# First mixer of a two-layer encoder: queries and keys of the next head traced ahead of the value products and the closing of a head, its values and scores behind them

## The chip, the cores and the metric

The kernel runs on one core of a Trainium2 chip. The metric is the device time of one execution in microseconds (us). The engines are TensorE (PE; its weight loads PEld), VectorE (DVE), ScalarE (ACT), GpSimd (POOL) and SyncE (SP), which here issues the transfers.

## The reference

An encoder of two layers, width 1024, runs on two sequences, a sample of 512 tokens and a prompt of 256, 768 tokens together. Each layer is a mixer and a convolutional feed-forward block, both with a conditioning (`adaln`) that scales, shifts and gates. The mixer of the first layer is a two-way mLSTM with 4 heads of 256 channels; the change is in it. Cut to what matters:

```python
proj = h @ w_in                       # q, k, v, o: 1024 channels each; 16 gate channels
s   = einsum('td,sd->ts', qc, kc) * exp(log_d - m_t)
num = einsum('ts,se->te', s, vc) + (state of earlier chunks)
den = sum(s) + (state of earlier chunks)
h   = num / maximum(abs(den), exp(-m_t))
hs  = h_fwd + h_bwd
hs  = hs * rsqrt(mean(hs * hs) + EPS) * head_g
return (hs * sigmoid(o)) @ w_out
```

All is computed in float32. The second layer has windowed attention as its mixer.

## The kernel before

**Precision.** Each float32 operand is split into a high and a low part (`fp_copy_split`, L232 to L240: ScalarE casts the high part, VectorE subtracts for the low one), and each product is three matmuls: high by high, high by low, low by high. Activations lie in `hh` and `hl` (tiles `zh`, `zl`), weights come as units of 256 output channels. `halves` (L257) loads a unit in two half-units of 128x1024 into the tag `raw` (5 buffers, L244) and splits them into `whi` and `wlo` (3 buffers each).

**Products.** `gemmT` (L265) makes 128 output channels of one half-unit for one sequence, channels on partitions: 24 matmuls of 512 columns for the sample, 24 of 256 for the prompt. `gemmN` (L308) makes values, tokens on partitions: 6 tiles of 24 matmuls. Both write PSUM banks of the tag `ps` (4 banks); scores, value products and transposes use the tag `pa` (4 banks).

**The mixer** (`mlstm`, L737). After the opening norm, the gates and the queries of head 0, a loop runs over the heads h (L795). For each it traces, in this order:

1. the masks `mb` (L797): two loads of gate rows on SP (L800) and two additions on POOL (L802);
2. the queries and keys (L808 to L822): two units, four half-units, eight calls of `gemmT`, evacuated by a split with or without a scale (`keep`, L753; ScalarE L236 or L239, VectorE L237 or L240);
3. the scores (L845 to L880): for each of 4 + 2 key blocks the products `S`, the weights `E` by ScalarE's exponentials (L864 to L868), VectorE's multiplications (L869, L870) and the split into `PT` (sample) or `nt` (prompt);
4. the values (`values`, L824): ahead of the scores in head 0, behind them in the others;
5. the closing (L887 to L932): the value products of scores and `v`; denominators (ACT L908, DVE L911 and L912); scaling and sum of the two directions (ACT L913, DVE L914); squares with a sum (ACT L916); the root by a power (DVE L918, POOL L919); the scaling by it (ACT L922); transposes (PE L926) and the evacuation into `hsT` (DVE L930).

Behind the loop four units of `o` are made by `gemmT`, put through a sigmoid (ACT L942), multiplied by `hsT` (POOL L943) and split into `ho` (L934 to L944). The output projection reads `ho`.

**Side work.** Two generators are advanced at fixed points: `fill` (L818, L832, L940), the conditioning of layer 1, whose step is two multiply-adds of 128x1024 on VectorE (L470, L472); and `fillp` (L820, L834, L890), that of layer 0, whose step is four matmuls of 256 columns with 32 weight columns. Both load rows of 512 KB into `raw`, and both take a `ps` bank for a group of eight rows.

**Memory.** `slab` (L220) is a tag of 6 buffers for the large tiles. While a head's scores run, its masks, queries, keys and values and one or two `hsT` tiles hold slabs.

**What sets the order.** A scheduler at build time (L1716, `schedule_with_timeline_sim=True`) puts the instructions of each engine into a fixed order, along a timeline that it simulates: of two instructions that are ready, the one that was traced first goes first. Where the code traces a step is thus its priority, and an instruction traced later can be put ahead of one that is not ready in the simulated timeline. `issue_after` (L842, L852) keeps head 0's scores behind its values. On the chip each engine works through its fixed order.

Of the kernel before, what the change touches and what calls it, by code (L numbers as in the profile page):

```python
# [10 lines left out]
F32 = mybir.dt.float32  # L11
R = mybir.dt.float32r
AF = mybir.ActivationFunctionType
ALU = mybir.AluOpType

P = 128
D = 1024
KC = D // P
T = 768
# [46 lines left out]
U_MIN = 0  # L66
# [79 lines left out]
class Net:  # L146
# [590 lines left out]
    def mlstm(self, pool, xt, rows, raws):  # L737
        nc, io = self.nc, self.io
        T6 = T // P
# [5 lines left out]
        F, a, M, z = (B[0:G, j] for j in range(4))  # L745
# [39 lines left out]
        aT = pool.tile([P, T6, G], F32, name="aT")  # L785
        eT = pool.tile([P, T6, G], F32, name="eT")

        def columns(src, dst):
            pt = self.pa()[:, : T6 * G]
            for t in range(T6):  # L790
                nc.tensor.transpose(pt[:, t * G : (t + 1) * G], src[:, t * P : (t + 1) * P], self.ident[0:G, 0:G])
            nc.vector.tensor_copy(dst, pt.rearrange("p (t g) -> p t g", g=G))

        hsT = [self.slab([P, 4, T]) for _ in range(2)]
        for h in range(4):  # L795

            mb = self.slab([P, 4, T])  # L797
            for d in range(2):
                r = d * 32 + h
                nc.sync.dma_start(mb[:, d], md[r : r + 1, :].to_broadcast([P, T]))  # L800
                mask = self.kct[:, (MF, MB)[d] : (MF, MB)[d] + P]
                nc.gpsimd.tensor_tensor(  # L802
                    mb[:, 2 + d].rearrange("p (t c) -> p t c", t=T6),
                    mb[:, d].rearrange("p (t c) -> p t c", t=T6),
                    mask.unsqueeze(1).to_broadcast([P, T6, P]),
                    ALU.add,
                )
            qk = []  # L808
            for i in range(2):
                if h == 0 and i == 0:  # L810
# [2 lines left out]
                t = self.slab([P, 2, 2, T], R)  # L813
# [5 lines left out]
                    if h:  # L819
                        self.step(self.fillp)  # L820
                qk.append(t)
            qt, kt = qk  # L822

            def values():  # L824
                v = self.slab([P, 2, T6, 258], R)
                nc.vector.memset(v[:, 0, :, 256:258].bitcast(F32), 1.0)
                nc.vector.memset(v[:, 1, :, 256:258].bitcast(F32), 0.0)

                def evac(t, o):
                    self.fp_copy_split(v[:, 0, t, :256], v[:, 1, t, :256], o)  # L830
                    if t % 2 == 0:
                        self.step(self.fill)  # L832
                    elif h:
                        self.step(self.fillp)  # L834

                self.gemmN(U_MIN + 3 * h + 2, evac)
                return v

            if h == 0:
                v = values()  # L840
                behind = self.last_mm
                with self.tc.issue_after(behind.ins):  # L842
                    columns(a, aT)

            pts = {}  # L845
            for q, (s0, s1) in enumerate(SEQS):
                n = (s1 - s0) // P
                for j in range(n):
                    kj = s0 // P + j
                    ks = slice(kj * P, (kj + 1) * P)  # L850
                    S = self.pa()[:, : s1 - s0]
                    with ExitStack() if h else self.tc.issue_after(behind.ins):  # L852
                        for c in range(2):
                            self.mm(S, kt[:, 0, c, ks], qt[:, 0, c, s0:s1], c == 0, False)
                            self.mm(S, kt[:, 0, c, ks], qt[:, 1, c, s0:s1], False, False)
                            self.mm(S, kt[:, 1, c, ks], qt[:, 0, c, s0:s1], False, c == 1)
# [14 lines left out]
                    if q == 0:  # L871
                        t = [pool.tile([P, 640], R, tag="PT", name=self.nm("PT"), bufs=8) for _ in range(2)]
# [3 lines left out]
                    else:  # L876
                        for d, cols in ((0, slice(nb, w)), (1, slice(0, nb))):
                            m = cols.stop - cols.start
                            pts[q, j, d] = [self.tmp([P, m], R) for _ in range(2)]
                            self.fp_copy_split(*pts[q, j, d], E[:, cols])  # L880
            if h:
                v = values()
            if h == 0:
                nc.vector.tensor_tensor(F, F, M, ALU.add)
                nc.scalar.activation(F, F, AF.Exp, scale=-1.0)
                columns(F, eT)
            ss = pool.tile([P, T6], F32, tag="ss", name=self.nm("ss"), bufs=2)  # L887
            for q, (s0, s1) in enumerate(SEQS):
                n = (s1 - s0) // P
# [2 lines left out]
                for i in range(n):  # L892
# [5 lines left out]
                    for d in range(2):  # L898
                        o = self.pa()[:, :258]
# [31 lines left out]
                        hsT[ch // 4][:, ch % 4, s0:s1], pt[:, : s1 - s0], self.cst(HG + ch), None, ALU.mult  # L931
                    )  # L932

        ho = [self.slab([P, 2, 2, T], R) for _ in range(4)]  # L934
        for u in range(4):
            for c, w in self.halves(U_MIN + 12 + u):
                ch = 2 * u + c
                for q, (s0, s1) in enumerate(SEQS):
                    o = self.gemmT(w, q)
                    self.step(self.fill)  # L940
                    sg = pool.tile([P, s1 - s0], F32, tag="E", name=self.nm("sg"), bufs=2)
                    nc.scalar.activation(sg, o, AF.Sigmoid)  # L942
                    nc.gpsimd.tensor_tensor(sg, sg, hsT[ch // 4][:, ch % 4, s0:s1], ALU.mult)  # L943
                    self.fp_copy_split(ho[u][:, 0, c, s0:s1], ho[u][:, 1, c, s0:s1], sg)  # L944
        return lambda k, s0, s1: (ho[k // 2][:, 0, k % 2, s0:s1], ho[k // 2][:, 1, k % 2, s0:s1])


# [782 lines left out]
```

## Time and profile before

| | |
|---|---|
| runs | 1902.64, 1899.25, 1902.51 us; median 1902.51 us |
| profiled execution | span 1900.1 us, the only time shown for it; 2.4 us below the median |
| TensorE, mean granted clock over the span | 0.983 |
| scores of head 0 to the last gated product | about 120 to 467 us |

Columns of a timeline row: start in us, busy us, engine, line, operation, out<-in, shape, count; in brackets the idle time before it and what ended it. `pa<-slab,PT` and `pa<-slab,nt` are value products of the closing, `ps<-zh,whi` a product of `gemmT`, `ps<-whi,zh` one of `gemmN`, `ps<-raw,silc` a step of `fillp`, `pa<-kct,hs` a transpose. Matmuls overlap, so the time of one is best read from the start of one to the start of the next.

### The profile page before, as it was taken

What the parts mean: (1) busy time and instruction counts of PE and PEld (TensorE: products, weight loads), DVE (VectorE), ACT (ScalarE), POOL (GpSimd) and SP (SyncE); (2) the same over time, 40 slices, a digit from 0 to 9 for tenths busy, and PEclk for the clock granted to TensorE, in tenths of its full rate; (3) what the DMA queues carried; (4) which work ended last, traced back from release to release, by engine and by line L of the source; (5) the groups of instructions that cost most, each with busy time, mean ns of one, the idle gap of its engine ahead of it and who ended that gap; (6) DMA issues with size and microseconds to landing.
All of it is one profiled execution on the core that took longest, in us unless ns stands there. A gap on an engine that the chain in (4) does not pass through costs nothing.

```text
span 1900.1 us, 29288 instructions
## 1 busy us (share of the span) xinstructions
PE 1812.0 (95%) x11354; PEld 1672.5 (88%) x11354; DVE 1413.8 (74%) x2310; ACT 920.9 (48%) x1849; POOL 491.0 (26%) x395
## 2 busy tenths in 40 slices
PE   7889999999999999999999999989989999999997
PEld 5787887888998999999999988879979999999996
DVE  4664776687589877777777768875998777777777
ACT  4633434343456444444444466773564444444443
POOL 3001000022013433333332303330133333333322
PEclk9888999999999999999999999999999999999998
DMA  8243655456412222222222321212222222222211
GB/s 321 66 141 113 210 166 165 153 167 199 144 55 89 67 67 67 67 67 67 67 67 79 112 81 48 84 58 90 78 78 77 68 67 67 67 67 67 67 34 67
DMA packets 64246, 184.49 MB, mean 97 GB/s; under 512 B 6167, under 2 KB 23831, under 8 KB 64108
## 3 DMA queue, kind: packets, MB, share of 16 engines
q1 hardware_dynamic: 64108, 182.63, 29.6%
q8 instruction: 89, 1.46, 0.3%
q14 instruction: 49, 0.40, 0.1%
HBM read 176.17 MB, written 6.43 MB: 96 GB/s over the span
## 4 chain that ended last, share of the span: by engine, by line
PE 76%; DVE 11%; issue 5%; ACT 4%; DMA 2%; POOL 2%; SPq 0%; POOLq 0%; ACTq 0%; DVEq 0%
PE pa L230 23%; PE ps L230 23%; PE ps L1252 10%; PE ps L1253 9%; PE ps L1254 9%; DVE wlo L237 2%; DMA bt<-brow 1%; DVE slab L690 1%; ACT t L1078 1%; DVE t L1069 1%; POOL nt L112 1%; DVE slab L1479 1%; DVE zl L1210 1%; DVE slab L1478 0%; DVE slab L237 0%
## 5 line engine op out<-in xcount | busy, mean ns | idle before, releaser
L236 ACT CAST whi<-raw 128x1024 fp32r<-128x1024 f32 x237 | 248.7, 1049 | 401.1 <-PE pa L230 200.3
L237 DVE TENSOR_TENSOR wlo<-raw,whi 128x1024 fp32r<-128x1024 f32 x237 | 330.7, 1395 | 113.5 <-ACT whi L236 112.8
L230 PE MATMUL pa<-slab,whi 128*128 128x256 f32 (+1 forms) x1472 | 344.8, 331 | 4.4 <-DVE slab L690 4.2
L230 PEld LDWEIGHTS pa<-slab,whi 128*128 128x128 f32 x1472 | 250.9, 188 | 31.4 <-DVE slab L690 5.8
L690 DVE SCALAR_TENSOR_TENSOR slab<-pa,mod,slab 128x256 f32<-128x256 f32 (+1 forms) x368 | 207.8, 592 | 67.5 <-PE pa L230 66.9
L230 PE MATMUL ps<-zh,whi 128*128 128x256 f32 (+2 forms) x688 | 233.6, 340 | 4.4 <-ACT whi L236 2.6
L230 PE MATMUL pa<-slab,wlo 128*128 128x256 f32 (+1 forms) x736 | 234.0, 330 | 0.0
L230 PE MATMUL ps<-zh,wlo 128*128 128x256 f32 (+2 forms) x688 | 228.6, 335 | 4.3 <-DVE wlo L237 4.3
L230 PE MATMUL ps<-zl,whi 128*128 128x256 f32 (+2 forms) x688 | 229.0, 334 | 1.6 <-DVE zl L536 0.9
L1252 PE MATMUL ps<-zh,whi 128*128 128x384 f32 x504 | 171.2, 340 | 14.3 <-ACT ps L1307 13.1
L1253 PE MATMUL ps<-zl,whi 128*128 128x384 f32 x504 | 169.8, 337 | 1.7 <-DVE zl L1210 1.7
L1254 PE MATMUL ps<-zh,wlo 128*128 128x384 f32 x504 | 169.0, 335 | 0.0
L230 PEld LDWEIGHTS pa<-slab,wlo 128*128 128x128 f32 x736 | 138.3, 188 | 13.0 <-DVE wlo L237 0.9
L230 PEld LDWEIGHTS ps<-zh,whi 128*128 128x128 f32 x688 | 132.7, 193 | 18.0 <-ACT whi L236 3.2
L230 PEld LDWEIGHTS ps<-zh,wlo 128*128 128x128 f32 x688 | 132.4, 192 | 15.1 <-DVE wlo L237 5.1
L230 PEld LDWEIGHTS ps<-zl,whi 128*128 128x128 f32 x688 | 132.5, 193 | 11.2 <-DVE zl L536 1.3
L1505 POOL TENSOR_TENSOR slab<-slab 128x772 f32<-128x772 f32 x44 | 83.3, 1893 | 206.7 <-DVE slab L1479 193.9
L1283 POOL TENSOR_TENSOR raw<-raw,raw 128x512 f32<-128x512 f32 x40 | 52.1, 1303 | 294.1 <-DVE wlo L237 244.1
L1478 DVE SCALAR_TENSOR_TENSOR slab<-slab,cstt,slab 128x771 f32<-128x771 f32 x88 | 105.3, 1199 | 26.9 <-ACT slab L1476 26.9
L1479 DVE SCALAR_TENSOR_TENSOR slab<-slab,cstt,slab 128x771 f32<-128x771 f32 x88 | 119.7, 1360 | 0.8
L472 DVE SCALAR_TENSOR_TENSOR ada<-raw,silc,ada 128x1024 f32<-128x1024 f32 x84 | 114.0, 1387 | 6.5 <-DMA raw<-in_adaln_w_dram 6.3
L1252 PEld LDWEIGHTS ps<-zh,whi 128*128 128x128 f32 x504 | 94.7, 188 | 22.2 <-ACT ps L1307 18.2
(309 smaller groups left out, 4182.4 us busy)
## 6 DMA issues: line engine op xcount, KB each, us to landing
raw<-in_w_dram SPq DMA_DIRECT2D x208, 512.0 KB, 3.7
raw<-in_adaln_w_dram SPq DMA_DIRECT2D x84, 512.0 KB, 4.4
slab<-in_x_dram SPq DMA_DIRECT2D x12, 512.0 KB, 7.6
slab<-in_adaln_w_dram SPq DMA_DIRECT2D x12, 512.0 KB, 10.9
slab<-mrows SPq DMA_DIRECT2D x8, 384.0 KB, 5.7
xs<-slab SPq DMA_DIRECT2D x6, 512.0 KB, 2.9
bt<-brow SPq DMA_DIRECT2D x16, 192.0 KB, 3.2
slab<-xs SPq DMA_DIRECT2D x6, 512.0 KB, 6.7
```

The lines of the kernel that those rows point to most:

```text
L230: self.last_mm = self.nc.tensor.matmul(out, lhsT, rhs, start=start, stop=stop)
L236: nc.scalar.copy(hi, src)
L237: return nc.vector.tensor_tensor(lo, src, hi.bitcast(F32), ALU.subtract)
L472: stt(acc[:, s], row, w, acc[:, s], ALU.mult, ALU.add)
L690: self.nc.vector.scalar_tensor_tensor(x, o, self.mod[l][:, gc + c, q : q + 1], x, ALU.mult, ALU.add)
L1252: mm(o, wh[:, k], hi[k], start=start and k == 0, stop=False, skip_group_check=True)
L1253: mm(o, wh[:, k], lo[k], start=False, stop=False, skip_group_check=True)
L1254: mm(o, wl[:, k], hi[k], start=False, stop=k == 3, skip_group_check=True)
L1283: tt(q[0], q[2], q[0], ALU.subtract)
L1478: stt(y[:, 1:], u[:, :-1], w(0), y[:, 1:], ALU.mult, ALU.add)
L1479: stt(y[:, :-1], u[:, 1:], w(2), y[:, :-1], ALU.mult, ALU.add)
L1505: nc.gpsimd.tensor_tensor(y, y, yrow[:, j], ALU.mult)
```

## The change

The loop body is cut into functions (`masks`, `queries`, `values`, `weighed` for the scores, `closed` for the closing, `gated` for one unit of `o`), and their order is written out at the end. Head 0's masks, queries, values and scores come first, as before. Then, for each head h: masks, queries and keys of head h+1 (for the last head the first gated unit in their place); the closing of head h; values of head h+1; scores of head h+1. So the queries and keys of head h+1 are traced ahead of the closing of head h, and the values of heads 1 to 3 ahead of their scores. The tiles `ho` are taken one by one. The steps of `fill` and `fillp` stay where they were inside the parts and move with them; their number is the same. No instruction is added or taken away.

```diff
@@ -792,8 +792,9 @@
             nc.vector.tensor_copy(dst, pt.rearrange("p (t g) -> p t g", g=G))
 
         hsT = [self.slab([P, 4, T]) for _ in range(2)]
-        for h in range(4):
-
+        ho = [None] * 4
+
+        def masks(h):
             mb = self.slab([P, 4, T])
             for d in range(2):
                 r = d * 32 + h
@@ -805,6 +806,10 @@
                     mask.unsqueeze(1).to_broadcast([P, T6, P]),
                     ALU.add,
                 )
+            return mb
+
+        def queries(h):
+
             qk = []
             for i in range(2):
                 if h == 0 and i == 0:
@@ -819,28 +824,24 @@
                     if h:
                         self.step(self.fillp)
                 qk.append(t)
-            qt, kt = qk
-
-            def values():
-                v = self.slab([P, 2, T6, 258], R)
-                nc.vector.memset(v[:, 0, :, 256:258].bitcast(F32), 1.0)
-                nc.vector.memset(v[:, 1, :, 256:258].bitcast(F32), 0.0)
-
-                def evac(t, o):
-                    self.fp_copy_split(v[:, 0, t, :256], v[:, 1, t, :256], o)
-                    if t % 2 == 0:
-                        self.step(self.fill)
-                    elif h:
-                        self.step(self.fillp)
-
-                self.gemmN(U_MIN + 3 * h + 2, evac)
-                return v
-
-            if h == 0:
-                v = values()
-                behind = self.last_mm
-                with self.tc.issue_after(behind.ins):
-                    columns(a, aT)
+            return qk
+
+        def values(h):
+            v = self.slab([P, 2, T6, 258], R)
+            nc.vector.memset(v[:, 0, :, 256:258].bitcast(F32), 1.0)
+            nc.vector.memset(v[:, 1, :, 256:258].bitcast(F32), 0.0)
+
+            def evac(t, o):
+                self.fp_copy_split(v[:, 0, t, :256], v[:, 1, t, :256], o)
+                if t % 2 == 0:
+                    self.step(self.fill)
+                elif h:
+                    self.step(self.fillp)
+
+            self.gemmN(U_MIN + 3 * h + 2, evac)
+            return v
+
+        def weighed(h, mb, qt, kt, behind=None):
 
             pts = {}
             for q, (s0, s1) in enumerate(SEQS):
@@ -849,7 +850,7 @@
                     kj = s0 // P + j
                     ks = slice(kj * P, (kj + 1) * P)
                     S = self.pa()[:, : s1 - s0]
-                    with ExitStack() if h else self.tc.issue_after(behind.ins):
+                    with self.tc.issue_after(behind.ins) if behind else ExitStack():
                         for c in range(2):
                             self.mm(S, kt[:, 0, c, ks], qt[:, 0, c, s0:s1], c == 0, False)
                             self.mm(S, kt[:, 0, c, ks], qt[:, 1, c, s0:s1], False, False)
@@ -878,12 +879,10 @@
                             m = cols.stop - cols.start
                             pts[q, j, d] = [self.tmp([P, m], R) for _ in range(2)]
                             self.fp_copy_split(*pts[q, j, d], E[:, cols])
-            if h:
-                v = values()
-            if h == 0:
-                nc.vector.tensor_tensor(F, F, M, ALU.add)
-                nc.scalar.activation(F, F, AF.Exp, scale=-1.0)
-                columns(F, eT)
+            return pts
+
+        def closed(h, pts, v):
+
             ss = pool.tile([P, T6], F32, tag="ss", name=self.nm("ss"), bufs=2)
             for q, (s0, s1) in enumerate(SEQS):
                 n = (s1 - s0) // P
@@ -931,8 +930,8 @@
                         hsT[ch // 4][:, ch % 4, s0:s1], pt[:, : s1 - s0], self.cst(HG + ch), None, ALU.mult
                     )
 
-        ho = [self.slab([P, 2, 2, T], R) for _ in range(4)]
-        for u in range(4):
+        def gated(u):
+            ho[u] = self.slab([P, 2, 2, T], R)
             for c, w in self.halves(U_MIN + 12 + u):
                 ch = 2 * u + c
                 for q, (s0, s1) in enumerate(SEQS):
@@ -942,6 +941,29 @@
                     nc.scalar.activation(sg, o, AF.Sigmoid)
                     nc.gpsimd.tensor_tensor(sg, sg, hsT[ch // 4][:, ch % 4, s0:s1], ALU.mult)
                     self.fp_copy_split(ho[u][:, 0, c, s0:s1], ho[u][:, 1, c, s0:s1], sg)
+
+        mb = masks(0)
+        qk = queries(0)
+        v = values(0)
+        behind = self.last_mm
+        with self.tc.issue_after(behind.ins):
+            columns(a, aT)
+        pts = weighed(0, mb, *qk, behind)
+        nc.vector.tensor_tensor(F, F, M, ALU.add)
+        nc.scalar.activation(F, F, AF.Exp, scale=-1.0)
+        columns(F, eT)
+        for h in range(4):
+            if h < 3:
+                mb = masks(h + 1)
+                qk = queries(h + 1)
+            else:
+                gated(0)
+            closed(h, pts, v)
+            if h < 3:
+                v = values(h + 1)
+                pts = weighed(h + 1, mb, *qk)
+        for u in range(1, 4):
+            gated(u)
         return lambda k, s0, s1: (ho[k // 2][:, 0, k % 2, s0:s1], ho[k // 2][:, 1, k % 2, s0:s1])
```

## The prediction

> **What bounds the kernel now.** I read the page first, for the engine that carries the span.
>
> ```profile
> PE 1812.0 (95%) x11354; PEld 1672.5 (88%) x11354; DVE 1413.8 (74%) x2310; ACT 920.9 (48%) x1849; POOL 491.0 (26%) x395
> ```
>
> TensorE is busy for 95% of the span. The change adds and removes no instruction, so the time can only move by the time in which TensorE waits, or runs at less than its full clock, in the stretch that is reordered. That stretch begins at about 120 us, with the scores of head 0, and ends at about 467 us, where the output projection begins. So I asked next for TensorE's waits in 120 to 467 us (columns: who waited for whom, us in total, times, longest).
>
> ```profile
> PE ps L230 <- DVE wlo L237: 4.3, 4, 2.3
> PE pa L926 <- ACT hs L922: 4.1, 1, 4.1
> PE ps L230 <- ACT whi L236: 2.6, 2, 1.4
> PE ps L487 <- ACT sb L484: 1.0, 1, 1.0
> PE ps L487 <- DVE sb L483: 0.6, 1, 0.6
> PE pa L230 <- DVE slab L930: 0.6, 1, 0.6
> PE ps L230 <- ACT sg L942: 0.5, 1, 0.5
> ```
>
> The seven rows add up to 13.7 us. That, with what the clock loses behind these waits, is all that an order of the work can win here: about 1% of the time. One wait stands out, the 4.1 us before a transpose of a closing (L926). The timeline of TensorE shows its place.
>
> ```profile
> 150.22 0.39 PE L230 MATMUL ps<-zh,wlo 128*128 128x512 f32 x1
> 150.45 0.39 PE L230 MATMUL ps<-zh,whi 128*128 128x512 f32 x1
> ...
> 152.27 0.39 PE L230 MATMUL ps<-zh,wlo 128*128 128x512 f32 x1
> 152.59 1.50 PE L230 MATMUL ps<-raw,silc 128*32 128x256 f32 x24
> 158.19 0.69 PE L926 MATMUL pa<-kct,hs 128*128 128x128 f32 x2 [4.11 <-ACT hs L922]
> ...
> 162.73 2.30 PE L230 MATMUL pa<-slab,nt 128*128 128x258 f32 x9 [0.63 <-DVE slab L930]
> ```
>
> Two things are to be seen. First, the products with `zh` up to 152.27 are projections of head 1 (gemmT), which TensorE runs between the value products of head 0: the scheduler already mixes the two, although the code before traces the queries of head 1 behind the closing of head 0. The change therefore turns a priority round, it does not open an overlap that was missing. Second, between 152.3 and 164.6 no projection runs; TensorE is left with the end of the closing and waits for it. The rows of ScalarE and VectorE in the same time say why.
>
> ```profile
> 154.22 0.84 ACT L913 ACTIVATE hs<-pa,dn 128x256 f32<-128x256 f32 x2 [3.63 <-DVE dn L912]
> ...
> 160.92 1.36 ACT L239 ACTIVATE slab<-ps 128x512 fp32r<-128x512 f32 x3
> ```
>
> ```profile
> 151.37 2.48 DVE L472 SCALAR_TENSOR_TENSOR ada<-raw,silc,ada 128x1024 f32<-128x1024 f32 x2 [0.37 <-DMA raw<-in_adaln_w_dram]
> 153.77 0.23 DVE L911 TENSOR_TENSOR dn<-dn,eT 128x2 f32<-128x2 f32 x2
> ```
>
> The closing's denominators (L911) stand on VectorE behind two conditioning sums (L472, 2.48 us), ScalarE waits for them 3.63 us at L913, and the three evacuations of head 1's query products (L239) stand in ScalarE's order behind the whole closing chain, until 160.92. There are four `ps` banks; with three full and the conditioning product in the fourth, no further projection could start.
>
> **The change part by part.** *Queries and keys of head h+1 traced ahead of the closing of head h.* Their evacuations now rank ahead of the closing's steps on ScalarE and VectorE, so banks come free while the closing's chain is under way, and TensorE has projections to run in place of the wait. What the wait costs today, in three windows (columns: window, length, then busy time of PE, PEld, DVE, ACT, POOL, the granted clock, DMA share, GB/s):
>
> ```profile
> 158.00:164.60 6.60, 5.78 (x25) 5.38 (x26) 3.01 (x7) 3.46 (x11) 3.15 (x2) 0.50 0.00 1
> 164.60:186.50 21.90, 21.90 (x135) 19.30 (x133) 4.98 (x15) 6.90 (x20) 4.41 (x3) 0.95 0.36 108
> 186.50:195.50 9.00, 9.00 (x52) 6.61 (x48) 8.28 (x16) 5.74 (x12) 0.00 (x0) 1.00 0.26 77
> ```
>
> The idle time is 4.11 + 0.63 us. In the next 6.60 us the clock is 0.50: of the 6.60 - 0.63 that are worked, half is lost, 3.0 us. In the 21.9 us after that the mean is 0.95, another 21.9 x 0.05 = 1.1 us. Together 4.11 + 0.63 + 3.0 + 1.1 = 8.8 us. I take all of it as gained, because the work that covers it, the rest of head 1's queries and its keys, is there at that time: it ran as soon as the banks were free, from 164.6 on. If that cover is missing in the new order, the 8.8 us stay (rivals A and D).
>
> *Queues that the moved steps pass.* The masks of head h+1 (two loads on SP at L800, two additions on POOL at L802) are now traced ahead of the closing of head h, whose power (L919) is also POOL's. These rows are of SP and of POOL:
>
> ```profile
> 151.41 14.45 SPq L800 DMA_DIRECT2D slab<-mrows  x4
> 157.57 3.58 POOL L802 TENSOR_TENSOR slab<-slab,kct 128x768 f32<-128x768 f32 x2
> ```
>
> On POOL the power can be held up by the two additions, 3.58 us at most, and TensorE, in a closing, waits for the power; I take nothing, since a slab for the mask is free by the time the scores of head h run, so that the additions can be done well ahead of the power. On SP four mask loads kept the queue for 14.45 us, until the closing of head 0 had released a slab, and loads of weights stood behind them. That can come out from nothing to 14.45 us better or worse for such a load; in the list of TensorE's waits none ends with a transfer, so I take 0.
>
> *Scores behind the values.* In row 186.50:195.50 the scores of head 1 ran nearly alone, with VectorE at 8.28 of 9.00 us, and the next product had its weights ready at once, because TensorE was busy for all of the 9.00 us. In the new order the projections of the next head stand behind the scores, in place of the values; either has 24 products a half-unit and the same weight splits. Cost 0; the bound either way is the 9.00 - 8.28 = 0.7 us that VectorE has left there, in each of three heads.
>
> *Projections without the closing among them.* This is the one part that I count against the change. With the closing behind them, the projections run denser, and VectorE has to keep up. What it does in a half-unit, from the groups of 294 to 350 us, where the queries and keys of head 3 ran with the closing of head 2 (the last columns are busy us, mean ns, and idle time):
>
> ```profile
> L472 DVE SCALAR_TENSOR_TENSOR ada<-raw,silc,ada 128x1024 f32<-128x1024 f32 x15 | 20.4, 1385 | 0.6 <-DMA raw<-in_adaln_w_dram 0.6
> L237 DVE TENSOR_TENSOR wlo<-raw,whi 128x1024 fp32r<-128x1024 f32 x6 | 7.3, 1220 | 4.2 <-ACT whi L236 4.2
> ...
> L240 DVE SCALAR_TENSOR_TENSOR slab<-ps,slab 128x512 fp32r<-128x512 f32 x2 | 1.4, 684 | 0.0
> ...
> L240 DVE SCALAR_TENSOR_TENSOR slab<-ps,slab 128x256 fp32r<-128x256 f32 x2 | 0.8, 416 | 0.0
> ```
>
> A half-unit needs 1.22 + 0.68 + 0.42 us, and from head 2 on two conditioning steps of two sums each, 4 x 1.385 = 5.54 us: 7.9 us of VectorE. TensorE needs 24 products of 512 columns at 0.23 us (150.22 to 150.45) and 24 of 256 at 0.12 us:
>
> ```profile
> 23.03 0.28 PE L230 MATMUL ps<-zh,wlo 128*128 128x256 f32 x1
> 23.15 0.28 PE L230 MATMUL ps<-zh,whi 128*128 128x256 f32 x1
> ```
>
> That is 24 x 0.35 = 8.4 us. So VectorE is at 7.9 of 8.4, 94%, before any closing step. What happens when it is full shows in 320 to 340 us:
>
> ```profile
> 294.30:349.60 55.30, 51.73 (x342) 42.92 (x335) 39.63 (x63) 21.65 (x58) 5.41 (x4) 0.97 0.66 211
> 320.00:340.00 20.00, 17.72 (x98) 14.88 (x96) 19.57 (x27) 7.98 (x20) 4.40 (x3) 0.91 0.71 224
> 329.90:333.00 3.10, 2.85 (x8) 2.23 (x9) 3.10 (x4) 0.00 (x0) 0.00 (x0) 0.62 0.76 247
> 333.00:336.50 3.50, 3.50 (x15) 2.83 (x14) 3.50 (x6) 1.40 (x3) 0.00 (x0) 0.85 0.56 192
> ```
>
> ```profile
> 330.15 0.50 PE L230 MATMUL ps<-zh,wlo 128*128 128x512 f32 x1 [2.28 <-DVE wlo L237]
> ```
>
> VectorE is busy for 19.57 of 20 us, a weight's low part comes late, and TensorE waits 2.28 us; over the whole stretch VectorE has 39.63 of 55.30 us. The clock falls behind this wait to 0.62 for 3.10 us and 0.85 for 3.50 us: 1.2 + 0.5 = 1.7 us more, 4.0 us in all. The projections of heads 2 and 3 run with the full conditioning; for these two I bound the added waits by 0 and by 2 x 4.0 = 8.0 us, and take one, 4.0 us, since the closing still takes TensorE's time in between where its operands are ready.
>
> [...]
>
> *The sum.* -8.8 + 4.0 = -4.8 us. The profiled execution has a span of 1900.1 us; the median of the three runs, 1902.5 us, is 2.4 us above it, which I leave as it is: 1900.1 - 4.8 + 2.4 = 1897.7 us. The last gated products, the projection behind them and the rest are the same instructions and I count no change there. About 0.2%, 3.8 us, is what a measurement of this kernel can tell from no change; the forecast lies just over it.
>
> **The rivals.**
>
> *A: the stall moves.* The closing of head h now runs among the values of head h+1, which are traced behind it, as the queries were. If the evacuations of the values come to stand behind the closing's chain on ScalarE, as L239 did until 160.92, the four banks fill there, and the 8.8 us come back once: 1902.5 us, no change. For it: the same engines and banks. Against it: the list of waits has the wait of L926 once, so three of the four closings go without it today, while the same banks serve them. [...]
>
> *B: the stall comes in two heads (slower).* The place is the transposes L926 of the closing, now traced behind all conditioning steps of the next head's queries. Each link of the chain through VectorE (L911, L914, L918) can stand behind a pair of sums as L911 did behind the 2.48 us at 151.37. It decides when TensorE reaches the transposes with no product ready, in two closings in place of one. That is one stall more than now: 1902.5 + 8.8 = 1911.3 us. Against it: the values, 144 products, are ready work.
>
> *C: the weight waits go too.* If the splits, traced earlier, come early enough, the 4.3 us of L237 and 2.6 us of L236 in the list of waits go as well, with 1.7 us of clock: -8.8 - 6.9 - 1.7 = -17.4, 1885.1 us. Against it: VectorE's 94%.
>
> *D: the order hardly changes,* because the scheduler mixes the parts anyway. Then the first stall stays: 1902.5 us. Against it: which of two ready steps goes first is just what the order of tracing decides.
>
> **How the numbers follow.** The forecast, between 0 and two added waits (1893.7 to 1901.7), has 0.45; A and D, no change, 0.23 together; B, and less than B, 0.20; C, or half of it, 0.12. The forecast lies with about 0.31 on the faster side of 1898.7, the rest within 0.2%; with C's 0.12 faster is 0.43. Same is 0.14 of the forecast and 0.20 of A and D, 0.34 in all; slower is B with the last 0.03 of A and D, 0.23. The range takes in half of C's additional gain and B's whole stall: 1888 to 1912. The forecast's own is 1893.7 to 1901.7.
>
> **What would show it right or wrong.** Right: in the changed profile the first waits of L926 on L922 are gone, the granted clock behind head 0's scores stays at 1.00, ScalarE evacuates head 1's queries (L239's step) before the closing's `hs` scaling (L922's), and VectorE is fuller among the projections of heads 2 and 3, with about one more wait on `wlo`. Wrong: a wait of 4 us or more of a transpose, or of the first product of a bank, among the values (A, B); no more waits on `wlo` at all (C); or TensorE's rows in the order of before (D). A move of the time that does not lie in 120 to 467 us would show that something outside of this reasoning changed.

## The result, and the profile after

| | median of runs, us | lowest to highest | ratio to before, 95% interval |
|---|---|---|---|
| before | 1901.55 | 1899.12 to 1906.30 (20 runs) | |
| changed | 1905.09 | 1901.75 to 1909.79 (20 runs) | 1.0016 [1.0009, 1.0024] |
| changed, in a second comparison | 1903.32, beside 1901.65 | 1898.47 to 1908.20 (12 runs) | 1.0004 [0.9991, 1.0017] |

The change makes the kernel slower by 3.5 us in the first comparison and by nothing that can be told in the second: its cost lies between nothing and 0.24%. Inside the predicted range, but on the other side of zero from the forecast of -4.8 us.

The profiled execution of the changed kernel has a span of 1903.6 us (before 1900.1) at a mean granted clock of 0.982 (0.983). The first row of the profile's page shows the engines as before:

```profile
PE 1813.7 (95%) x11354; PEld 1674.9 (88%) x11354; DVE 1412.7 (74%) x2310; ACT 921.6 (48%) x1849; POOL 496.3 (26%) x395
```

TensorE's waits in the changed kernel from 120 to 467 us (who waited for whom, us in total, times, longest):

```profile
PE pa L925 <- ACT hs L921: 4.8, 2, 2.4
PE pa L791 <- DVE E L871: 2.8, 1, 2.8
PE ps L230 <- DVE slab L237: 2.1, 1, 2.1
PE ps L487 <- DVE sb L483: 0.6, 1, 0.6
PE ps L230 <- ACT sg L941: 0.5, 1, 0.5
PE pa L230 <- DVE slab L831: 0.5, 1, 0.5
PE ps L435 <- DVE sb L431: 0.4, 1, 0.4
PE ps L230 <- DVE wlo L237: 0.3, 1, 0.3
PE ps L230 <- ACT whi L236: 0.2, 1, 0.2
PE ps L230 <- DMA raw<-in_adaln_w_dram: 0.2, 1, 0.2
```

(In the changed kernel's numbers L925 is the closing's transpose and L921 the scaling of `hs`, which were L926 and L922; L791 is the transpose in `columns`, L871 the masking of E in the scores.) The ten rows add up to 12.4 us, against 13.7 before. Nearly every row is another one. The waits for weights are gone, 4.3 us for `wlo` and 2.6 us for `whi` before, 0.3 and 0.2 now. In their place stand two waits of 2.4 us before the transposes of a closing, one of 2.8 us before the columns of eT, and one of 2.1 us for an evacuation.

The stall of head 0 did go. The stretch of 146 to 170 us, first before and then after (window, length, busy us of PE, PEld, DVE, ACT, POOL, granted clock, DMA share, GB/s):

```profile
146.00:170.00 24.00, 19.26 (x125) 16.99 (x124) 10.69 (x27) 11.67 (x39) 6.38 (x5) 0.79 0.45 126
```

```profile
146.00:170.00 24.00, 24.00 (x165) 19.81 (x164) 5.10 (x9) 3.95 (x10) 0.00 (x0) 1.00 0.17 49
```

TensorE was idle for 24.00 - 19.26 = 4.7 us and at 0.79 of its clock; now it is busy for all of the 24 us at full clock. ScalarE's rows of the changed kernel in 148 to 166 us say how: they are evacuations alone, and nothing of the closing stands among them.

```profile
148.73 0.39 ACT L239 ACTIVATE slab<-ps 128x256 fp32r<-128x256 f32 x1 [1.63 <-PE ps L230]
154.98 0.59 ACT L236 CAST slab<-ps 128x512 fp32r<-128x512 f32 x1 [5.87 <-PE ps L230]
...
164.10 0.59 ACT L236 CAST slab<-ps 128x512 fp32r<-128x512 f32 x1 [5.88 <-PE ps L230]
```

So the gain came and was given back. Cut at the first score of head 0 and at the first product of the output projection, and counted to the start of TensorE's last product, 7.4 us ahead of the end in both, the two profiled executions divide like this (us; the last two columns add up, from the trace's record of the granted clock, the time at half clock in the second and the third part):

| | until the first score | first mixer | behind it | half clock, mixer | half clock, behind |
|---|---|---|---|---|---|
| before | 120.2 | 346.7 | 1425.8 | 17.1 | 9.0 |
| changed | 121.0 | 344.4 | 1430.8 | 13.7 | 15.7 |

0.8 - 2.3 + 5.0 = 3.5 us, the difference of the spans. In the mixer the waits fell by 1.3 us and the half clock by 3.4 us, which is about 1.7 us of lost work: 3.0 us together, where 2.3 were measured. The other two parts the prediction had left alone. Both are looked at below.

**Where the new waits come from.** TensorE of the changed kernel from 256 to 268 us, in the closing of head 1 (start, duration, last column idle time and releaser):

```profile
256.35 0.28 PE L230 MATMUL ps<-zh,wlo 128*128 128x256 f32 x1
256.56 1.07 PE L230 MATMUL ps<-raw,silc 128*32 128x256 f32 x16
257.56 2.07 PE L230 MATMUL pa<-slab,PT 128*128 128x258 f32 x15
...
263.75 0.69 PE L925 MATMUL pa<-kct,hs 128*128 128x128 f32 x2 [2.41 <-ACT hs L921]
264.09 2.28 PE L230 MATMUL pa<-slab,nt 128*128 128x258 f32 x9
...
267.30 0.56 PE L230 MATMUL ps<-whi,zh 128*128 128x256 f32 x1
```

The last projection of head 2 is done at 256.6. Up to 261.3 TensorE has the conditioning and the weighted sums, and then nothing but transposes, which wait for `hs`. The first value product runs at 267.30, when the stall is over. Why no earlier is told by the load of its weights on SP and by ScalarE:

```profile
257.26 0.81 SPq L245 DMA_DIRECT2D raw<-in_w_dram  x2
```

```profile
263.18 1.71 ACT L921 ACTIVATE hs<-hs,ss 128x256 f32<-128x256 f32 x4 [1.32 <-POOL ss L918]
264.80 1.03 ACT L236 CAST whi<-raw 128x1024 fp32r<-128x1024 f32 x1
```

The loads were issued at 257.3 us, after the projections had ended, and the cast of the first weights comes at 264.80, behind the chain that it should have covered. ScalarE's rows of the closing of head 2 have the same order, the scaling of `hs` at 347.90 and the cast at 349.52 us. What such a wait costs beside itself, in two windows of the changed kernel:

```profile
262.40:269.20 6.80, 5.45 (x29) 4.67 (x29) 3.34 (x4) 3.71 (x8) 0.75 (x1) 0.52 0.49 155
347.70:351.10 3.40, 2.63 (x13) 2.64 (x14) 0.52 (x1) 3.19 (x7) 0.17 (x1) 0.54 0.98 360
```

Waits of 2.41 and 2.36 us brought 6.8 and 3.4 us at about half clock (0.52 and 0.54 in these rows).

### The profile page after: what moved, and what is told of

It reads as the page before. It is cut to its first block, busy times and chain, and to the rows that moved or that the text cites. A ratio compares the mean times of both kernels' runs of the same rounds, so it can differ in the third digit from the quotient of the medians.

```text
span 1903.6 us, 29287 instructions
## 1 busy us (share of the span) xinstructions
PE 1813.7 (95%) x11354; PEld 1674.9 (88%) x11354; DVE 1412.7 (74%) x2310; ACT 921.6 (48%) x1849; POOL 496.3 (26%) x395
## 5 line engine op out<-in xcount | busy, mean ns | idle before, releaser
L237 DVE TENSOR_TENSOR wlo<-raw,whi 128x1024 fp32r<-128x1024 f32 x237 | 332.3, 1403 | 113.4 <-ACT whi L236 112.5
L230 PE MATMUL pa<-slab,whi 128*128 128x256 f32 (+1 forms) x1472 | 347.1, 333 | 4.6 <-DVE slab L690 4.4
L230 PEld LDWEIGHTS pa<-slab,whi 128*128 128x128 f32 x1472 | 252.7, 190 | 31.5 <-DVE slab L690 6.1
L230 PE MATMUL pa<-slab,wlo 128*128 128x256 f32 (+1 forms) x736 | 235.0, 331 | 0.1
L230 PE MATMUL ps<-zh,whi 128*128 128x256 f32 (+2 forms) x688 | 232.0, 338 | 1.9 <-ACT zh L534 1.0
L230 PE MATMUL ps<-zl,whi 128*128 128x256 f32 (+2 forms) x688 | 227.3, 331 | 1.3 <-DVE zl L536 0.9
L230 PE MATMUL ps<-zh,wlo 128*128 128x256 f32 (+2 forms) x688 | 227.2, 331 | 0.3 <-DVE wlo L237 0.3
L230 PEld LDWEIGHTS pa<-slab,wlo 128*128 128x128 f32 x736 | 139.4, 190 | 13.1 <-DVE wlo L237 0.9
L230 PEld LDWEIGHTS ps<-zh,whi 128*128 128x128 f32 x688 | 131.3, 191 | 16.3 <-issue 4.4
L230 PEld LDWEIGHTS ps<-zh,wlo 128*128 128x128 f32 x688 | 131.3, 191 | 11.0 <-DVE slab L237 0.8
L230 PEld LDWEIGHTS ps<-zl,whi 128*128 128x128 f32 x688 | 131.4, 191 | 10.4 <-DVE zl L536 1.3
L472 DVE SCALAR_TENSOR_TENSOR ada<-raw,silc,ada 128x1024 f32<-128x1024 f32 x84 | 112.9, 1376 | 8.4 <-DMA raw<-in_adaln_w_dram 8.4
## 6 DMA issues: line engine op xcount, KB each, us to landing
slab<-in_adaln_w_dram SPq DMA_DIRECT2D x12, 512.0 KB, 10.2
```

The source lines that it names most:

```text
L230: self.last_mm = self.nc.tensor.matmul(out, lhsT, rhs, start=start, stop=stop)
L237: return nc.vector.tensor_tensor(lo, src, hi.bitcast(F32), ALU.subtract)
L472: stt(acc[:, s], row, w, acc[:, s], ALU.mult, ALU.add)
```

## The experiments

**The theory.** The moved projections are all used up by the time a closing needs cover; the only cover left there is the next head's values, and their weights come too late, since their loads are traced behind the closing and the load buffers (five `raw`) go in the order of tracing. **Rivals.** That the closing's own chain, filled with conditioning steps, is too long for any cover; that putting the scores behind the values costs the time; and that the time is lost outside of the mixer and has nothing to do with it. Every diff below is against the changed kernel; every ratio is to the kernel before, run on the same chip in turn.

**again: the changed kernel once more.** No edit.

> The changed kernel once more, for a second profile. Theory F (filler used up: the projections of the next head are all done before the closing, so the closing's transposes at L925 wait for their own chain while the values' weights are not yet there): the same waits in the mixer, about 2.4 us each before the transposes of heads 1 and 2 and 2.8 us at L791, and the stretch from head 0's scores to the last gated product again 345 us, give or take 1. Theory L (the loss lies behind the mixer, where short waits that both kernels have bring half-clock visits or not, by where they fall in time): the half-clock visits behind 545 us differ from the 13.7 us of the first profile, while the mixer's stretch is the same; time 1903 to 1907 us.

Measured: 1903.32 us beside 1901.65, ratio 1.0004 [0.9991, 1.0017]; mixer 344.7 us, half clock in it 10.2 us and behind it 15.1. The mixer repeats to 0.3 us.

**e1: the values' weights loaded and split ahead of the closing.**

```diff
-        for _, (hi, lo) in self.halves(u):
+        for _, (hi, lo) in parts or self.halves(u):
...
                 qk = queries(h + 1)
+                parts = list(self.halves(U_MIN + 3 * h + 5))
...
-                v = values(h + 1)
+                v = values(h + 1, parts)
```

> The two half-units of the values of head h+1 are loaded and split ahead of the closing of head h, nothing else is moved. Theory F: the values are ready when the projections are used up, the waits before the transposes of heads 1 and 2 (2.4 + 2.4 us), the one of 2.06 us among head 1's values and the half-clock behind them (13.7 us at half, 6.8 us lost) go; 8 to 12 us faster than the changed kernel, 5 to 9 us faster than the kernel before. Theory L: the waits in the mixer are not what counts, within 2 us of the changed kernel. A third theory (VectorE is too full in the projections): the waits only change place, within 3 us of the changed kernel, with waits on wlo.

Measured: 1894.39 us beside 1901.65, ratio 0.9960 [0.9946, 0.9973], clear of the repeat's interval. The mixer took 332.2 us, 12.2 less than in the changed kernel, with no time at half clock. The waits in 75 to 470 us of e1:

```profile
...
PE pa L925 <- ACT hs L921: 1.0, 3, 0.4
...
```

The transposes wait 1.0 us in place of 4.8, and the evacuation's wait of 2.1 us is gone too. The missing cover was the cause of these waits.

**e8: only the loads ahead, the splits where they were.**

```diff
                 qk = queries(h + 1)
+                early = [self.load(U_MIN + 3 * h + 5, i) for i in range(2)]
...
-                v = values(h + 1)
+                v = values(h + 1, [(i, self.split(w)) for i, w in enumerate(early)])
```

> The changed kernel with only the loads of the values' half-units ahead of the closing; their splits stay behind it. If theory F is right about the raw buffers (the loads wait behind the closing's conditioning rows), most of the gain of the first experiment is here too, 4 to 8 us faster than before. If it is ScalarE's order (the cast of the high part behind the closing's chain) that makes the values late, the waits of about 2.4 us before the transposes stay and the time is that of the changed kernel, 1902 to 1906 us.

Measured: 1894.02 us (6 runs) beside 1902.28, ratio 0.9949 [0.9936, 0.9962]. The mixer took 335.4 us, with 3.4 at half clock. SP, ScalarE and TensorE of e8 at the place of the stall:

```profile
245.86 0.80 SPq L245 DMA_DIRECT2D raw<-in_w_dram  x2
```

```profile
250.60 1.05 ACT L236 CAST whi<-raw 128x1024 fp32r<-128x1024 f32 x1 [2.47 <-DMA raw<-in_w_dram]
252.14 1.06 ACT L236 CAST whi<-raw 128x1024 fp32r<-128x1024 f32 x1 [0.49 <-DMA raw<-in_w_dram]
...
262.81 1.71 ACT L921 ACTIVATE hs<-hs,ss 128x256 f32<-128x256 f32 x4 [1.32 <-POOL ss L918]
```

```profile
260.32 0.36 PE L230 MATMUL ps<-whi,zh 128*128 128x256 f32 x1
...
265.77 0.28 PE L230 MATMUL ps<-wlo,zh 128*128 128x256 f32 x1
265.89 0.38 PE L925 MATMUL pa<-kct,hs 128*128 128x128 f32 x2
```

```profile
262.40:269.20 6.80, 6.80 (x61) 6.25 (x60) 5.89 (x8) 2.68 (x8) 0.38 (x1) 1.00 0.56 175
```

The loads go out at 245.9 in place of 257.3 us, and the casts follow by themselves at 250.6 and 252.1. The scaling of `hs` starts at 262.81, no earlier to speak of than the 263.18 of the changed kernel: the chain is as long as it was. But value products run from 260.32 to 265.77, the transposes follow without a wait, and the clock stays at 1.00. So it was the cover and not the chain, and of the cover the load. By the runs, moving the two loads gives all that e1 gave (the intervals overlap); by the profiles it gives 9.0 of e1's 12.2 us in the mixer, with 3.2 us of waits left before the transposes of other closings.

**e6: e1 with the scores ahead of the values again.**

```diff
-                v = values(h + 1, parts)
                 pts = weighed(h + 1, mb, *qk)
+                v = values(h + 1, parts)
```

> The changed kernel with the values' half-units loaded and split ahead of the closing, and with the scores ahead of the values as in the kernel before. Theory F: with the values ready as filler the order of the two matters little, within 2 us of the first experiment (1892 to 1897 us, 0.3 to 0.5% faster than before). If the values ahead of the scores cost 5 us by themselves, as the run of that half alone may say, 4 us or more faster than the first experiment.

Measured: 1897.45 us beside 1902.28, ratio 0.9977 [0.9966, 0.9989]; mixer 332.7 us, against 332.2 in e1. Which of the two comes first does not matter to the mixer once the weights are there; the intervals of e1 and e6 overlap.

**e2: the values ahead of the scores alone; queries and keys behind the closing, as before.**

```diff
         for h in range(4):
+            closed(h, pts, v)
             if h < 3:
                 mb = masks(h + 1)
                 qk = queries(h + 1)
-            else:
-                gated(0)
-            closed(h, pts, v)
-            if h < 3:
                 v = values(h + 1)
                 pts = weighed(h + 1, mb, *qk)
-        for u in range(1, 4):
+        for u in range(4):
             gated(u)
```

> Half of the change alone: the values ahead of the scores, but the closing of head h ahead of the queries of head h+1 as before, and no gated unit ahead of the last closing. Theory F: the projections follow the closing, so its chain has filler, and no 2.4 us wait of the transposes of heads 1 and 2; between the kernel before and 6 us faster. If the values ahead of the scores cost by themselves (scores bare between values and the closing that needs them), 3 us or more slower than before, with waits of the closing's first products.

Measured: 1906.49 us beside 1901.65, ratio 1.0028 [1.0016, 1.0040]; mixer 346.1 us. Waits of e2 in 75 to 470 us:

```profile
...
PE ps L230 <- ACT whi L236: 4.5, 3, 1.9
PE pa L925 <- ACT hs L921: 4.3, 1, 4.3
PE ps L230 <- DVE wlo L237: 1.7, 2, 1.4
...
```

The stall of 4.3 us is that of head 0, back as in the kernel before, and the waits for weights remain. This half of the change brings nothing. The runs are 0.28% slower, but the mixer does not show where: its 346.1 us lie within the 343.4 to 346.9 us of the four profiles of the kernel before (below).

**e3: the queries and keys ahead alone; scores ahead of values, as before.**

```diff
-                v = values(h + 1)
                 pts = weighed(h + 1, mb, *qk)
+                v = values(h + 1)
```

> The other half alone: queries and keys ahead of the closing (and the first gated unit ahead of the last one), but the scores ahead of the values as before. Theory F: the transposes of the closings wait as in the changed kernel, since the values' weights come as late or later, 2 to 6 us slower than the kernel before; if the order of scores and values is what costs, as fast as the kernel before or faster.

Measured: 1903.85 us beside 1901.65, ratio 1.0012 [0.9997, 1.0026]; mixer 344.4 us, that of the changed kernel. Waits of e3 in 75 to 470 us:

```profile
PE ps L230 <- DVE slab L237: 12.0, 2, 10.1
PE pa L925 <- ACT hs L921: 4.6, 2, 2.4
PE pa L791 <- DVE E L871: 2.7, 1, 2.7
...
```

These are the changed kernel's waits, so the queries and keys ahead bring both the gain and the new stalls. The time itself, between no change and 0.26% slower, can't be told from either kernel.

**e9: the conditioning steps of the closings of heads 0 to 2 taken behind the values.**

```diff
-                self.step(self.fillp, 2)
+                if h == 3:
+                    self.step(self.fillp, 2)
...
                 v = values(h + 1)
+                self.step(self.fillp, 4)
```

> The changed kernel with the four conditioning steps (fillp) of the closings of heads 0 to 2 traced behind the values of the next head, in place of inside the closing; loads of the values' weights stay behind the closing. If the values' weights come late because rows of conditioning traced ahead of them take the raw buffers (the part of theory F that the load-only experiment points to), they come earlier here too: the waits before the transposes shrink, and 3 to 8 us faster than the changed kernel (1896 to 1902 us). If the place in SP's order behind the closing is what makes them late, or only the rows of fill matter, within 2 us of the changed kernel (1902 to 1907 us).

Measured: 1898.97 us beside 1900.43, ratio 0.9996 [0.9983, 1.0010]; mixer 339.2 us. Waits of e9 in 75 to 480 us, without the 10.1 us of head 0's values:

```profile
...
PE ps L230 <- DMA raw<-in_adaln_w_dram: 3.8, 1, 3.8
PE pa L791 <- DVE E L871: 2.6, 1, 2.6
...
```

No transpose of these closings waits any more. SP, ScalarE and TensorE of e9 in the closing of head 1 tell why (L922 is here the scaling of `hs`, L926 the transpose):

```profile
246.00 0.81 SPq L245 DMA_DIRECT2D raw<-in_w_dram  x2
```

```profile
250.76 1.05 ACT L236 CAST whi<-raw 128x1024 fp32r<-128x1024 f32 x1 [0.43 <-DMA raw<-in_w_dram]
...
268.26 1.71 ACT L922 ACTIVATE hs<-hs,ss 128x256 f32<-128x256 f32 x4
```

```profile
257.55 0.28 PE L230 MATMUL ps<-whi,zh 128*128 128x256 f32 x1
...
271.15 0.38 PE L926 MATMUL pa<-kct,hs 128*128 128x128 f32 x2
```

It is not a shorter chain: the scaling starts at 268.26, later than the 263.18 of the changed kernel. The values' weights are loaded at 246.0 in place of 257.3 us although their loads are still traced behind the closing, and value products run from 257.55 on. So the rows of conditioning that are traced ahead of these loads, and that take `raw` buffers and SP's turn, are what made them late. In the changed kernel six such rows went out on SP from 240.25 to 251.90 us, and the first of the two loads then waited 5.3 us, until conditioning products (L230) ended at about 257.2 us. The mixer is 5.2 us shorter than in the changed kernel, in spite of a new wait of 3.8 us for a row of conditioning (at 285 us). The runs can't be told from the kernel before; by the ratios they are 1.5 to 3.8 us faster than those of the changed kernel.

**e4: the first gated product no longer ahead of the last closing.**

```diff
-            else:
-                gated(0)
             closed(h, pts, v)
...
-        for u in range(1, 4):
+        for u in range(4):
```

> The changed kernel without the first gated unit ahead of the last closing. Theory F: a gated unit is the only filler that head 3's closing can have, since no values follow; without it in front the gated products follow the closing and fill its chain, as the queries did before. Within 2 us of the changed kernel either way (1902 to 1907 us), and no wait of head 3's transposes in either; if the gated unit in front is what costs, 3 us or more faster than the changed kernel.

Measured: 1907.37 us beside 1900.43, ratio 1.0035 [1.0022, 1.0048], 0.31% above the ratio of the repeat and clear of its interval, though not of the first comparison's (up to 1.0024); mixer 346.6 us, 2.2 more than in the changed kernel. Waits of e4 in 75 to 480 us:

```profile
...
PE pa L925 <- ACT hs L921: 4.7, 2, 2.4
...
PE ps L230 <- ACT whi L236: 1.6, 2, 1.4
...
```

The stalls of the two closings stay, and waits for weights come on top (1.6 us against 0.2). So the gated product in front is, as far as this tells, a part of the change that helps.

**e10: e8, with the columns of eT just ahead of the closing of head 0.** The wait of 2.8 us at L791 was left in e8 (2.2 us): the transposes of `columns` need a `pa` bank that the scores release only when L871 is done, and that stands behind a conditioning sum on VectorE (in the changed kernel the two sums of L472 at 133.31 us, 2.48 us long; then L871 at 136.91 and the transposes at 137.48).

```diff
-        columns(F, eT)
         for h in range(4):
...
+            if h == 0:
+                columns(F, eT)
             closed(h, pts, v)
```

> The kernel with the early loads of the values' weights (second batch), and the transposes of F into eT (L791) traced just ahead of head 0's closing, behind the queries and keys of head 1, in place of ahead of them. The transposes wait 2.2 to 2.8 us for a pa bank in every changed profile. If that wait counts, it goes, with a half-clock visit in some runs: 2 to 5 us faster than the early loads alone (1889 to 1892 us). If another stands behind it (the bank is still late, or the closing's denominators then wait for eT), within 1 us of 1894 us.

Measured: 1888.99 us beside 1900.43 (6 runs, 1885.68 to 1893.79), ratio 0.9934 [0.9914, 0.9954]. Waits of e10 in 120 to 467 us:

```profile
PE pa L925 <- ACT hs L921: 2.5, 3, 1.8
PE ps L230 <- ACT whi L236: 1.1, 1, 1.1
...
```

The wait at L791 is gone. This version beats both kernels; against e8 the intervals overlap, so that the last step's own share is not shown.

**b2, b3, b4: the kernel before, three more profiles.** No edit. They are for the part behind the mixer.

> The kernel before, unchanged, for a second profile. In the five profiles with a changed order the part behind the mixer takes 3 to 5 us more than in the one profile of the kernel before (1428.8 to 1430.8 against 1425.8 us), most of it at about 1057 us, where the clock halved behind a wait of 0.95 us that all six have. Theory L (by chance of when the wait falls): this profile has that visit or another in its place, and 1427 to 1431 us behind the mixer. If the changed order does something lasting (where tiles lie, transfers), the part takes 1425 to 1426.5 us again with full clock at 1057.

> The kernel before, a third profile, with the same expectations as for the second: 1427 to 1431 us behind the mixer by theory L, 1425 to 1426.5 us if the changed order does something lasting there. In the mixer, both: a wait of the transposes of head 0 of about 4 us.

> The kernel before, a fourth profile. So far the part behind the mixer takes 1425.8, 1426.3 and 1428.5 us in it, with 9.0 to 11.9 us at half clock, and 1427.5 to 1431.8 us in ten profiles with a changed order, with 11.7 to 15.7 us at half clock. If the changed order has lasting more half-clock visits there, this profile lies at 1425 to 1428.5 us with under 12 us at half clock; if it is chance, it may as well lie at 1429 to 1431 us with 13 us or more.

Measured, each once: 1899.34, 1903.25 and 1906.46 us. The four profiles of the kernel before take 343.4 to 346.9 us in the mixer and 1425.8 to 1428.5 behind it (mean 1427.1, of these 10.4 at half clock). The two of the changed kernel take 344.4 and 344.7 in the mixer and 1430.8 and 1429.4 behind it (mean 1430.1, 15.4 at half clock). So of the change's cost the mixer shows none: its mean of 344.6 is 1.0 us below that of before, and within the spread of the four. Behind it stand 3.0 us, of which (15.4 - 10.4) / 2 = 2.5 us are the clock.

That part has the same instructions in either kernel, and TensorE's waits in it add up to between 40.3 and 42.0 us in the four profiles of before and to 42.1 and 41.0 us in the two of the changed kernel. What differs is what follows a wait. The same wait of 1 us in the first profile of each kernel, before and then changed:

```profile
1057.85 1.50 PE L230 MATMUL pa<-inv,nt 128*128 128x2 f32 x12 [0.97 <-POOL nt L112]
```

```profile
1057.00:1060.50 3.50, 2.65 (x23) 2.65 (x24) 0.87 (x3) 0.56 (x2) 1.44 (x2) 1.00 0.61 203
1060.50:1064.00 3.50, 3.50 (x33) 3.50 (x32) 2.81 (x7) 2.33 (x6) 2.50 (x4) 1.00 0.27 99
```

```profile
1056.94 1.84 PE L230 MATMUL pa<-inv,nt 128*128 128x2 f32 x12 [0.95 <-POOL nt L112]
```

```profile
1056.00:1059.50 3.50, 2.56 (x16) 2.56 (x17) 0.64 (x2) 0.67 (x2) 1.25 (x3) 0.78 0.61 211
1059.50:1063.00 3.50, 3.50 (x18) 3.50 (x18) 1.11 (x3) 0.83 (x2) 1.27 (x3) 0.50 0.00 1
```

0.97 us of waiting left the clock at 1.00; 0.95 us took it to 0.78 and then 0.50. In the 3.50 us behind it TensorE got through 33 products in the one and 18 in the other. These are two executions, and this wait does not tell the two kernels apart: it lasts 0.93 to 0.98 us in all 14 profiles, and the clock halves behind it in 12 of them, b2, b3 and b4 among them, but not in the first profile of the kernel before and not in `again`.

Why the changed orders fall into half clock more often there is not settled. Ten profiles of changed orders, experiments among them, have 14.3 us of it behind the mixer in the mean (11.7 to 15.7), the four of before 10.4 (9.0 to 11.9). Yet e10, with 15.6 us of it, takes 1427.5 us for that part, and an experiment that shifts the whole part in time without changing the mixer was not tried.

## Why the prediction was wrong, point by point

*Head 0's stall, -8.8 us.* Right in mechanism and place: 146 to 170 us runs at full clock without idle time. The sign named for it, evacuations of head 1 ahead of the closing on ScalarE, is in the rows of 148 to 166 us.

*"I take all of it as gained, because the work that covers it ... is there at that time."* This is the step that failed. For head 0 it held. But the same projections were until then the cover of the other closings, and pulled ahead they were used up before those closings came. Rival B had the stall in two closings, and was put aside with "the values, 144 products, are ready work". They were not ready: the prediction had not asked when their weights would land. The loads went out at 257.3 us, the first value product ran at 267.30 us, and the transposes waited 2.41 and 2.36 us, with 6.8 and 3.4 us at half clock behind them. B's mechanism came about at some six tenths of its size, each stall being 2.4 us long in place of 4.1; its path was another, the missing cover rather than the links of the chain on VectorE. The two stalls cost 4.8 us of waiting and, of 10.2 us at half clock, up to 5.1 us: about the 8.8 us that head 0 had given. Experiment e1 shows it by moving loads and splits, e8 by moving the loads alone, e9 by taking away the rows that held the loads; with the loads early (e8) the kernel is faster, as forecast.

*The columns of eT and the evacuation.* 2.8 us at L791 and 2.1 us at L237 in the scores and values of the first heads were in no term. The first goes when `columns` moves (e10), the second when the values' weights are loaded early (e1, e8).

*Denser projections, +4.0 us.* Wrong in sign. VectorE did not fill up in the mixer: it was busy for 226.8 us in 120 to 467 against 236.0 before, as 8.3 us of its work moved ahead of 120 us (75.5 us there against 67.1), and the waits for `wlo` and `whi` fell from 6.9 to 0.5 us. That was rival C's part of the story, against which VectorE's 94% had been held. That the moved work is why these waits fell is not shown: in e1 VectorE is busy for 235.3 us in that window, and the waits are 1.4 us.

*Scores behind the values, 0.* Right as far as it can be told: e1 and e6 differ by 0.5 us in the mixer, and without the queries ahead (e2) the mixer is no different from before.

*The queues, 0.* Wrong for SP, though not through the masks: the time at which two loads could go out set these stalls (e8, e9), and the queue was set to 0 because "in the list of TensorE's waits none ends with a transfer". A late load showed as a wait for ScalarE (L925 for L921, 2.41 us), since the transposes were what TensorE had at its head: the first value product, at 267.30 us, came behind them.

*What lay outside.* The prediction took no change ahead of 120 us and behind 467. Ahead, the wait of head 0's first values grew from 8.9 to 10.1 us: on VectorE a first weight split of head 1 (at 99.54 us, 1.20 us long) now stands ahead of the evacuations there, which fits the 1.2 us but was not tried by itself. Behind, 3.0 us by the means of the profiles came on top, mostly of the clock. The sign set for this, "a move of the time that does not lie in 120 to 467 us", is what was seen. So the failed step explains why the gain of 4.8 us did not come: the mixer itself, at -1.0 us by the means, would have given no change. That the kernel came out slower rests on the part behind the mixer, and why the clock is lower there stays open.

## What to carry to other kernels

Work that is to cover a stall is ready only when its operands have landed (here, with the loads out at 257.3 us, the first value product ran at 267.30; with the loads out at 245.9, in e8, value products ran from 260.32): ask for each candidate when its load is issued, and what holds the buffer that the load needs. Pulling work forward to cover one stall takes it away from the next, as here (4.1 us gone at head 0, 2.41 and 2.36 us come at the two closings behind it); follow the reordered engine to the end of the stretch and see what is left at each wait. If the cover lacks only its load, move the load, or the loads that take its buffers: moving two loads a head ahead turned a change of +0.04 to +0.16% into one of -0.5%.

## What the runs showed of the hardware

- In the traces' record of the granted clock, in the first profiles of the kernel before and of the changed kernel, the stretches at half clock lasted 3.41 us (six in each), 6.83 us (none and two), 10.24 us (two and one) or 13.65 us (one in each), but for the one at the end of the kernel (11.67 and 11.40 us). In these two profiles all changes of the clock, up and down, lie a whole number of steps of 3.4133 us apart, to within 0.004 us. The time at half clock was not in proportion to the wait: in the changed kernel 6.83 us of it came with a wait of 2.41 us and 6.83 us with one of 0.95 us, 3.41 us with one of 2.36 us.
- Whether a wait starts such a stretch depends on more than its length: at the same instruction 0.97 us started none in the first profile of the kernel before (clock 1.00 in the 3.50 us behind it) and 0.95 us started one in the changed kernel (0.50); of the 14 profiles, with 0.93 to 0.98 us of this wait, 12 had one, among them b2, which is the same kernel as before, and `again`, the changed kernel once more, had none. What decides it is open.
- The clock goes with part of the scatter between runs of one kernel: over 76 runs of the kernel before, time and mean granted clock are correlated at -0.68. The mean granted clock is 0.9831 over the 32 runs of the changed kernel and 0.9848 over these 76; the difference of 0.0017, times 1900 us, is 3.2 us, about what the two differ by. The runs are from several comparisons and scatter much, so that it is a hint and no proof.
